# The gate products of a two-layer mixer encoder: seven products in another order, with common sums copied into a second PSUM bank

## The chip, the cores and the metric

The kernel runs on one core of one Trainium2 chip. The metric is the device time of one execution in microseconds (us). The kernel before takes 2005.57 us, the median of 3 runs (2004.29 to 2006.87). One more execution was profiled; all rows below are from it.

## The reference, cut to what matters

Two layers follow one another. In each, `h` is the normalised input (1024 tokens of 1024 channels), four branches give `y_n`, and each branch is weighted by its own gate, a full 1024 x 1024 product with a bias and a sigmoid:

```python
for n, y in enumerate(branch_outs):                     # 4 branches
    y_n = (y * gate_paths[:, :, n]) @ w_branch[n]
    mg = jax.nn.sigmoid(h @ w_gate[n] + b_gate[n])
    merged = mg * y_n if merged is None else merged + mg * y_n
return x + merged @ w_out
```

## The kernel before, in words

All data lie transposed: channels on the 128 partitions, tokens along the free axis, in two halves of 512 tokens (`hf` 0 and 1). A fp32 product is made from three passes: each operand is split into a high and a low part by `split` (ACT copies the high part, DVE subtracts it from the source, lines 104 and 105), and `passes` (line 128) issues high-high, high-low and low-high matmuls of 128 x 128 weights on 512 columns.

`gates` (line 1007) computes the four gate products of a layer. Its outer loop runs over four pairs of output chunks (`dp`), its inner loop over the four branches (`n` in `ORDER`): 16 iterations in a layer, 32 in the kernel. An iteration makes a 2 x 2 block of results (two chunks `d` by two token halves `hf`) by a scheme of Strassen's kind, in the form of Winograd: seven products over four 128-row blocks each in the place of eight. So an iteration has 7 x 4 x 3 = 84 matmuls. The right operands are made once in a layer: `b11`, `b21` and `b22` are parts of `h`, and `tf[1]` to `tf[4]` (called t1 to t4 below) are differences of those parts, made by `token_forms` (t1 and t2 in tiles of tag `M`, t3 in tag `A`, t4 in tag `H`; `h` has tag `H` too). The left operands are made anew in each iteration by the generator `weight_forms` (line 974): two loads of 512 KB (`raw`), sums and differences by DVE (line 981), and a split of each of the seven forms into a `wf` tile, of which there are 6. `product` (line 1022) takes the forms from a list that is kept six ahead of TensorE.

Each iteration has three PSUM banks, G, A and B, taken in one iteration from the pool `mm` (3 banks) and in the next from `aux` (5 banks). The order of the products is

- b11 into G; ACT copies G to `p1` (line 1046)
- t2 into A; DVE adds `p1` to `c6`
- b21 onto G; result (0,0) is read from G
- t1 onto A; DVE adds `p1` to `c65`
- t3 into B; DVE adds B to `c65`, which is result (1,1)
- b22 onto A; DVE adds A to `p1`, which is result (0,1)
- t4 onto B; DVE adds B to `c6`, which is result (1,0)

`weigh` (line 1032) takes a result through the sigmoid (ACT, line 1035), multiplies it with the tile of `y` (DVE) and adds it to the sum over the branches (DVE; not in the first iteration of a `dp`). After a `dp`, `m` is stored through the POOL queue; the last `dp` stays on the chip as the tail. `out_proj` follows: `merged` reads `m` back (`mt`), splits it chunk by chunk (tile `m`, lines 104 and 105), and the products `op` begin with the first token half. The list scheduler of the framework sets the order on each engine, from program order and from what is ready; DMAs and weight loads are raised in priority.

Of the kernel before, what the change touches and what calls it, by code (L numbers as in the profile page):

```python
# [11 lines left out]
AF = mybir.ActivationFunctionType  # L12
ALU = mybir.AluOpType

P = 128
# [30 lines left out]
class Net:  # L46
# [931 lines left out]
    def weight_forms(self, l):  # L978

        nc = self.nc  # L980
        op = lambda o, a, b, f: nc.vector.tensor_tensor(out=o, in0=a, in1=b, op=f)
        flip = 0
        for dp in range(4):
            for n in ORDER:
                raw = self.raw(), self.spare(flip)
                flip = 1 - flip
                ys = [self.slot(f"y{d}", tag="A") for d in range(2)]
                with self.tc.high_priority(offset=AHEAD):
                    for r, d in zip(raw, range(2)):
                        nc.sync.dma_start(out=r, in_=self.a["w_gate"][l, n, 2 * dp + d])  # L990
                    for y, d in zip(ys, range(2)):
                        nc.gpsimd.dma_start(out=y, in_=self.y[l][n, 2 * dp + d])
                a11, a12, a21, a22 = raw[0][:, 0:4], raw[0][:, 4:8], raw[1][:, 0:4], raw[1][:, 4:8]
                yield self.weight_form(a11), ys
                s1, s2 = (self.t2(f"s{j}").rearrange("p (k n) -> p k n", n=P) for j in (1, 2))
                op(s1, a21, a22, ALU.add)
                op(s2, s1, a11, ALU.subtract)
                yield self.weight_form(s2), ys
                yield self.weight_form(a12), ys
                yield self.weight_form(s1), ys  # L1000
                op(a11, a11, a21, ALU.subtract)
                yield self.weight_form(a11), ys
                op(a12, a12, s2, ALU.subtract)
                yield self.weight_form(a12), ys
                yield self.weight_form(a22), ys

    def gates(self, l, tf):

        nc = self.nc
        b11, b21 = [self.h[k] for k in range(4)], [self.h[4 + k] for k in range(4)]  # L1010
        b22 = [[self.h[4 + k][1]] for k in range(4)]
        add = lambda o, a, b: nc.vector.tensor_tensor(out=o, in0=a, in1=b, op=ALU.add)
        flip = 0
        forms, made = self.weight_forms(l), []
        for dp in range(4):
            acc = None
            for i, n in enumerate(ORDER):
                bank = (self.mm, self.aux)[flip]
                flip = 1 - flip
                G, A, B = bank("g"), bank("ga"), bank("gb")  # L1020

                def product(ps, x, first):
                    while len(made) < LEAD:
                        f = next(forms, None)
                        if f is None:
                            break
                        made.append(f)
                    w, ys = made.pop(0)
                    self.passes(ps, [((w[0][:, k], w[1][:, k]), xk[0]) for k, xk in enumerate(x)], True, first, True)
                    return ys  # L1030

                def weigh(c, d, hf, src=None):

                    y = ys[d][:, hf * H:hf * H + H]
                    nc.scalar.activation(out=c, in_=c if src is None else src, func=AF.Sigmoid,
                                         bias=self.p(l, C_BG + 8 * n + 2 * dp + d))
                    if i == 0:
                        nc.vector.tensor_tensor(out=y, in0=y, in1=c, op=ALU.mult)
                    else:
                        nc.vector.tensor_tensor(out=c, in0=y, in1=c, op=ALU.mult)  # L1040
                        a = acc[d][:, hf * H:hf * H + H]
                        add(a, a, c)

                ys = product(G, b11, True)
                p1 = self.t2("p1")
                nc.scalar.activation(out=p1, in_=G, func=AF.Copy)
                product(A, tf[2], True)
                c6 = self.t2("c6")
                add(c6, A, p1)
                product(G, b21, False)  # L1050
                c11 = self.t2("c11")
                weigh(c11, 0, 0, G)
                product(A, tf[1], False)
                c65 = self.t2("c65")
                add(c65, A, p1)
                product(B, tf[3], True)
                add(c65, B, c65)
                weigh(c65, 1, 1)
                product(A, b22, False)
                add(p1, A, p1)  # L1060
                weigh(p1, 0, 1)
                product(B, tf[4], False)
                add(c6, B, c6)
                weigh(c6, 1, 0)
                if i == 0:
                    acc = ys
            if dp < 3:
                for d in range(2):
                    nc.gpsimd.dma_start(out=self.m[l][2 * dp + d], in_=acc[d])
        return acc  # L1070
# [200 lines left out]
```

## Time and profile before

| | before |
|---|---|
| median of 3 runs | 2005.57 us |
| the profiled execution | 2007.35 us |
| its span, from first to last instruction | 2005.6 us |
| TensorE matmul busy | 1967.1 us, 98% of the span |
| VectorE (DVE) busy | 1486.6 us, 74% |
| ScalarE (ACT) busy | 1000.5 us, 50% |

How to read it: a matmul's busy time holds its way through the array, so that successive matmuls overlap and a row's busy time is longer than its share of the stream. The pace is read from the distance of starts. In a row of the timeline, the first number is the start, the second the time from the first start to the last end of the group, `xN` the number of instructions; in square brackets stand the idle time before it and what ended that.

### The profile page before, as it was taken

How to read it: one execution, taken by the hardware profiler on the slowest of the kernel's cores; microseconds unless marked ns; L12 is line 12 of the kernel's file. 1: busy time of each engine (PE TensorE's matmuls, PEld its weight loads, DVE VectorE, ACT ScalarE, POOL GpSimd, SP SyncE). 2: the span in 40 equal slices, each digit the busy share in tenths (PEclk: the TensorE clock that was granted, in tenths of full speed). 3: DMA queues.
4: the chain of work that ended last, by engine and by line, in shares of the span. 5: the costliest groups of instructions: out<-in, count | busy, mean ns of one | idle time of the engine just before them, and what ended most of it. 6: DMA issues, size and time to landing. Idle time of an engine off the chain costs nothing.

```text
span 2005.6 us, 26782 instructions
## 1 busy us (share of the span) xinstructions
PE 1967.1 (98%) x9484; PEld 1625.6 (81%) x9484; DVE 1486.6 (74%) x2740; ACT 1000.5 (50%) x1917; POOL 41.1 (2%) x90
## 2 busy tenths in 40 slices
PE   8999999999999999999999999999999999999997
PEld 6777887887888888887888888888888888888887
DVE  7598878886577777776655888888564877777775
ACT  6335655567574334344421456656775643443441
POOL 0000000000000000000000000000000000000000
PEclk9999999999999999999999999999999999999999
DMA  7244343423774333427421534433248723424443
GB/s 236 77 149 118 108 123 115 127 72 101 265 270 170 135 106 106 156 73 258 157 86 45 158 116 126 131 108 108 82 147 294 274 86 124 135 98 146 166 150 106
DMA packets 129446, 281.08 MB, mean 140 GB/s; under 512 B 32928, under 2 KB 37920, under 8 KB 129312
## 3 DMA queue, kind: packets, MB, share of 16 engines
q1 hardware_dynamic: 118368, 239.52, 37.1%
q0 software_dynamic: 10944, 39.85, 5.9%
q8 instruction: 75, 1.23, 0.3%
q14 instruction: 59, 0.48, 0.1%
HBM read 186.84 MB, written 67.30 MB: 127 GB/s over the span
## 4 chain that ended last, share of the span: by engine, by line
PE 82%; DVE 9%; ACT 4%; DMA 3%; issue 2%; SPq 0%; DVEq 0%; ACTq 0%
PE z L128 25%; PE ga L128 13%; PE g L128 9%; PE op L128 8%; PE gb L128 8%; PE py L128 8%; PE z L255 3%; DVE cv L848 2%; PE pv L128 2%; PE s L465 1%; PE pt L491 1%; DVE w L105 1%; DMA mt<-m 1%; ACT o L522 1%; DVE p L474 1%
## 5 line engine op out<-in xcount | busy, mean ns | idle before, releaser
L128 PE MATMUL z<-h,w 128*128 128x512 f32 x3000 | 744.3, 397 | 2.5 <-DVE gp L609 1.4
L128 PEld LDWEIGHTS z<-h,w 128*128 128x128 f32 x3000 | 546.7, 188 | 111.4 <-DVE gp L609 1.8
L105 DVE TENSOR_TENSOR w<-wr,w 128x1024 fp32r<-128x1024 f32 (+1 forms) x135 | 158.7, 1179 | 109.4 <-ACT w L104 99.6
L104 ACT ACTIVATE w<-wr 128x1024 fp32r<-128x1024 f32 (+1 forms) x135 | 137.7, 1022 | 175.9 <-PE z L128 80.9
L128 PE MATMUL ga<-t,wf 128*128 128x512 f32 x768 | 189.0, 395 | 0.0
L128 PE MATMUL gb<-t,wf 128*128 128x512 f32 x768 | 187.8, 393 | 0.0
L128 PE MATMUL g<-h,wf 128*128 128x512 f32 x768 | 187.1, 393 | 0.0
L128 PE MATMUL op<-m,w 128*128 128x512 f32 (+1 forms) x960 | 181.2, 349 | 2.2 <-DVE m L105 2.2
L128 PE MATMUL py<-g,w 128*128 128x512 f32 x768 | 181.0, 395 | 0.6 <-DVE gp L609 0.5
L848 DVE SCALAR_TENSOR_TENSOR cv<-cv,params 128x512 f32<-128x512 f32 x240 | 179.4, 747 | 2.3
L128 PEld LDWEIGHTS op<-m,w 128*128 128x128 f32 x960 | 153.7, 188 | 28.1 <-DVE m L105 3.5
L128 PEld LDWEIGHTS ga<-t,wf 128*128 128x128 f32 x768 | 144.4, 188 | 33.8
L128 PEld LDWEIGHTS gb<-t,wf 128*128 128x128 f32 x768 | 144.4, 188 | 33.1
L128 PEld LDWEIGHTS py<-g,w 128*128 128x128 f32 x768 | 143.2, 188 | 34.0 <-ACT sg L608 0.9
L128 PEld LDWEIGHTS g<-h,wf 128*128 128x128 f32 x768 | 144.4, 188 | 32.4
L104 ACT ACTIVATE wf<-wr 128x512 fp32r<-128x512 f32 x144 | 90.9, 631 | 131.7 <-issue 48.3
L105 DVE TENSOR_TENSOR wf<-wr,wf 128x512 fp32r<-128x512 f32 x144 | 99.0, 688 | 21.9 <-ACT wf L104 20.8
L479 ACT ACTIVATE p<-p,nm 128x256 f32<-128x256 f32 (+2 forms) x192 | 87.9, 459 | 42.9 <-DVE nm L476 42.5
L128 PE MATMUL ga<-h,wf 128*128 128x512 f32 x384 | 94.2, 395 | 0.0
L104 ACT ACTIVATE wf<-s 128x512 fp32r<-128x512 f32 x64 | 40.5, 632 | 106.7 <-PE gb L128 64.1
L522 ACT ACTIVATE o<-pv 64x128 f32<-64x128 f32 x192 | 67.6, 352 | 48.6 <-PE pv L128 46.7
L128 PEld LDWEIGHTS ga<-h,wf 128*128 128x128 f32 x384 | 72.4, 188 | 16.7
(244 smaller groups left out, 2683.6 us busy)
## 6 DMA issues: line engine op xcount, KB each, us to landing
wr<-in_w_in_dram SPq DMA_DIRECT2D x75, 512.0 KB, 3.8
y<-y SPq DMA_DIRECT2D x128, 256.0 KB, 4.1
y<-y POOLq DMA_DIRECT2D x64, 512.0 KB, 4.8
wr<-in_w_gate_dram SPq DMA_DIRECT2D x48, 512.0 KB, 4.4
wr<-in_w_out_dram SPq DMA_DIRECT2D x32, 512.0 KB, 3.6
rot<-rt SPq DMA_DIRECT2D x192, 64.0 KB, 2.0
cv<-in_w_gate_dram SPq DMA_DIRECT2D x16, 512.0 KB, 4.8
wr<-in_w_branch_dram SPq DMA_DIRECT2D x16, 512.0 KB, 4.5
```

What stands on the lines that cost most here:

```text
L104: self.nc.scalar.activation(out=hi, in_=src, func=AF.Copy)
L105: self.nc.vector.tensor_tensor(out=lo, in0=src, in1=hi.bitcast(F32), op=ALU.subtract)
L128: self.nc.tensor.matmul(ps, w, x, start=(first and i + u == 0), stop=(i == n - 1 and u == 2), skip_group_check=open_)
L255: self.nc.tensor.matmul(ps, a[:, k], b, start=(k + j == 0), stop=(k == KC - 1 and j == 2))
L465: mm(s[i][h], q[h + j][:, qs], k[h][:, a:a + n], start=(j == 0), stop=(j == 2))
L474: nc.vector.tensor_tensor_reduce(out=p[:, h * 256:h * 256 + n], in0=s[h], in1=mask, scale=0.125, scalar=-3.0e38, op0=ALU.add, op1=ALU.max, ...
L479: nc.scalar.activation(out=ph, in_=ph, func=AF.Exp, bias=nm[:, h:h + 1], accum_out=st[:, t, 2 + h:3 + h])
L491: nc.tensor.transpose(pt[:rows[ci], cs], p[:, off:off + rows[ci]], self.ident)
L522: nc.scalar.activation(out=dst, in_=src, func=AF.Copy)
L848: self.tc.keep_in_program_order(nc.vector.scalar_tensor_tensor(out=y, in0=u[:, j:j + H], scalar=tap(j), in1=y, op0=ALU.mult, op1=ALU.add))
```

## The change

The seven products have another order and other banks. X, Y and V come from `mm` in each iteration; `aux` is not used here. ACT copies the sum in X into bank Y, and further matmuls accumulate on Y; the five DVE additions that joined partial sums become two, and ACT gets two more copies. The order after is

- b11 into X; ACT copies X to Y
- t3 into V; ACT copies V to `v7`
- t2 onto Y; ACT copies Y to `u2`
- t4 onto V; DVE adds V to `u2`, which is result (1,0)
- t1 onto Y; DVE adds Y to `v7`, which is result (1,1)
- b21 onto X; result (0,0) is read from X
- b22 onto Y; result (0,1) is read from Y

`weight_forms` yields the forms in the order of the products, and a11 - a21 gets a tile of its own (`s3`) in the place of a11.

```diff
                 a11, a12, a21, a22 = raw[0][:, 0:4], raw[0][:, 4:8], raw[1][:, 0:4], raw[1][:, 4:8]
+                s1, s2, s3 = (self.t2(f"s{j}").rearrange("p (k n) -> p k n", n=P) for j in (1, 2, 3))
                 yield self.weight_form(a11), ys
-                s1, s2 = (self.t2(f"s{j}").rearrange("p (k n) -> p k n", n=P) for j in (1, 2))
+                op(s3, a11, a21, ALU.subtract)
+                yield self.weight_form(s3), ys
                 op(s1, a21, a22, ALU.add)
                 op(s2, s1, a11, ALU.subtract)
                 yield self.weight_form(s2), ys
+                yield self.weight_form(a22), ys
+                yield self.weight_form(s1), ys
                 yield self.weight_form(a12), ys
-                yield self.weight_form(s1), ys
-                op(a11, a11, a21, ALU.subtract)
-                yield self.weight_form(a11), ys
                 op(a12, a12, s2, ALU.subtract)
                 yield self.weight_form(a12), ys
-                yield self.weight_form(a22), ys
...
-        flip = 0
...
-                bank = (self.mm, self.aux)[flip]
-                flip = 1 - flip
-                G, A, B = bank("g"), bank("ga"), bank("gb")
+                X, Y, V = self.mm("g"), self.mm("ga"), self.mm("gb")
...
-                ys = product(G, b11, True)
-                p1 = self.t2("p1")
-                nc.scalar.activation(out=p1, in_=G, func=AF.Copy)
-                product(A, tf[2], True)
-                c6 = self.t2("c6")
-                add(c6, A, p1)
-                product(G, b21, False)
+                copy = lambda o, a: nc.scalar.activation(out=o, in_=a, func=AF.Copy)
+                ys = product(X, b11, True)
+                copy(Y, X)
+                product(V, tf[3], True)
+                v7 = self.t2("v7")
+                copy(v7, V)
+                product(Y, tf[2], False)
+                u2 = self.t2("u2")
+                copy(u2, Y)
+                product(V, tf[4], False)
+                add(u2, V, u2)
+                weigh(u2, 1, 0)
+                product(Y, tf[1], False)
+                add(v7, Y, v7)
+                weigh(v7, 1, 1)
+                product(X, b21, False)
                 c11 = self.t2("c11")
-                weigh(c11, 0, 0, G)
-                product(A, tf[1], False)
-                c65 = self.t2("c65")
-                add(c65, A, p1)
-                product(B, tf[3], True)
-                add(c65, B, c65)
-                weigh(c65, 1, 1)
-                product(A, b22, False)
-                add(p1, A, p1)
-                weigh(p1, 0, 1)
-                product(B, tf[4], False)
-                add(c6, B, c6)
-                weigh(c6, 1, 0)
+                weigh(c11, 0, 0, X)
+                product(Y, b22, False)
+                c12 = self.t2("c12")
+                weigh(c12, 0, 1, Y)
```

## Rows read from the trace of the kernel before

**Rows 1.** The page, part 1: busy time (us), share of the span and number of instructions of an engine.

```profile
PE 1967.1 (98%) x9484; PEld 1625.6 (81%) x9484; DVE 1486.6 (74%) x2740; ACT 1000.5 (50%) x1917; POOL 41.1 (2%) x90
```

**Rows 2.** Busy time by stretch, for the gate stage of layer 0 and of layer 1. The columns are the stretch, its length, then busy time and number of instructions of PE, PEld, DVE, ACT and POOL, then the granted clock (1.00 is full speed), the DMA share and GB/s.

```profile
605.90:917.96 312.06, 312.06 (x1346) 253.06 (x1344) 236.40 (x362) 126.77 (x196) 17.77 (x34) 1.00 0.38 130
1590.70:1900.10 309.40, 309.40 (x1345) 252.39 (x1344) 235.78 (x362) 126.50 (x196) 17.66 (x34) 1.00 0.38 129
```

**Rows 3.** Groups of matmuls of the gate stage (first from the page, over both layers: busy time, mean ns of one, idle time of PE before them), and below them the one wait of PE in the seams behind it, from the waits over the whole span (total, times, longest).

```profile
L128 PE MATMUL ga<-t,wf 128*128 128x512 f32 x768 | 189.0, 395 | 0.0
...
L128 PE MATMUL g<-h,wf 128*128 128x512 f32 x768 | 187.1, 393 | 0.0
...
PE op L128 <- DVE m L105: 2.2, 2, 1.2
```

**Rows 4.** The timeline of PE, one iteration in the middle of layer 0, product by product (b11, t2, b21, t1, t3, b22, t4) and the b11 of the next iteration.

```profile
781.41 2.96 PE L128 MATMUL g<-h,wf 128*128 128x512 f32 x12
784.21 2.96 PE L128 MATMUL ga<-t,wf 128*128 128x512 f32 x12
787.01 2.91 PE L128 MATMUL g<-h,wf 128*128 128x512 f32 x12
789.76 2.95 PE L128 MATMUL ga<-t,wf 128*128 128x512 f32 x12
792.55 2.93 PE L128 MATMUL gb<-t,wf 128*128 128x512 f32 x12
795.32 2.96 PE L128 MATMUL ga<-h,wf 128*128 128x512 f32 x12
798.12 2.96 PE L128 MATMUL gb<-t,wf 128*128 128x512 f32 x12
800.92 2.96 PE L128 MATMUL g<-h,wf 128*128 128x512 f32 x12
```

**Rows 5.** The same for an iteration in the middle of layer 1.

```profile
1745.37 2.91 PE L128 MATMUL g<-h,wf 128*128 128x512 f32 x12
1748.12 2.95 PE L128 MATMUL ga<-t,wf 128*128 128x512 f32 x12
1750.90 2.91 PE L128 MATMUL g<-h,wf 128*128 128x512 f32 x12
1753.66 2.95 PE L128 MATMUL ga<-t,wf 128*128 128x512 f32 x12
1756.44 2.93 PE L128 MATMUL gb<-t,wf 128*128 128x512 f32 x12
1759.21 2.92 PE L128 MATMUL ga<-h,wf 128*128 128x512 f32 x12
1761.97 2.91 PE L128 MATMUL gb<-t,wf 128*128 128x512 f32 x12
1764.72 2.91 PE L128 MATMUL g<-h,wf 128*128 128x512 f32 x12
```

**Rows 6.** The timeline of PE at the beginning of the gate stage of layer 0: the last product of the branches (`py`), then the first b11, t2 and b21.

```profile
599.68 6.39 PE L128 MATMUL py<-g,w 128*128 128x512 f32 x27
605.90 2.92 PE L128 MATMUL g<-h,wf 128*128 128x512 f32 x12
608.66 2.95 PE L128 MATMUL ga<-t,wf 128*128 128x512 f32 x12
611.45 2.91 PE L128 MATMUL g<-h,wf 128*128 128x512 f32 x12
```

**Rows 7.** Groups of instructions of the gate stage of layer 0 (605.7 to 917.7 us), for durations: busy time, mean ns of one, and idle time before them with what ended it. They are the copy of G to SBUF, the sigmoid read from PSUM, a high part of a weight form, and a weight form's sum.

```profile
L1046 ACT ACTIVATE p<-g 128x512 f32<-128x512 f32 x16 | 9.6, 597 | 19.0 <-PE g L128 18.9
L1035 ACT ACTIVATE c<-g,params 128x512 f32<-128x512 f32 x16 | 11.0, 689 | 32.6 <-PE g L128 32.6
L104 ACT ACTIVATE wf<-s 128x512 fp32r<-128x512 f32 x32 | 20.2, 632 | 53.4 <-PE gb L128 32.1 <-DVE s L981 21.3
L981 DVE TENSOR_TENSOR s<-s,wr 128x512 f32<-128x512 f32 x15 | 10.3, 685 | 0.0
```

**Rows 8.** The timeline of ACT and DVE within the iteration of rows 4: the copy of G after b11, and the addition that reads A after t1.

```profile
784.41 0.60 ACT L1046 ACTIVATE p<-g 128x512 f32<-128x512 f32 x1 [1.35 <-PE g L128]
...
793.70 0.68 DVE L1012 TENSOR_TENSOR c<-ga,p 128x512 f32<-128x512 f32 x1
```

**Rows 9.** The timeline at the seam from the gates to `out_proj`: PE in layer 0 and in layer 1, then DVE in layer 0.

```profile
917.96 4.78 PE L128 MATMUL op<-m,w 128*128 128x512 f32 x20
923.75 26.60 PE L128 MATMUL op<-m,w 128*128 128x512 f32 x113 [1.01 <-DVE m L105]
...
1900.14 4.81 PE L128 MATMUL op<-m,w 128*128 128x512 f32 x20
1906.17 43.93 PE L128 MATMUL op<-m,w 128*128 128x512 f32 x205 [1.22 <-DVE m L105]
...
916.97 0.68 DVE L1012 TENSOR_TENSOR p<-ga,p 128x512 f32<-128x512 f32 x1
...
920.03 0.68 DVE L1012 TENSOR_TENSOR c<-gb,c 128x512 f32<-128x512 f32 x1
920.64 0.68 DVE L1012 TENSOR_TENSOR y<-y,p 128x512 f32<-128x512 f32 x1
...
923.01 0.68 DVE L105 TENSOR_TENSOR m<-mt,m 128x512 fp32r<-128x512 f32 x1
```

## The prediction

> **What bounds the kernel now.** I read first the page's busy shares: TensorE's matmuls fill 98% of the span, DVE 74%, ACT 50% [rows 1]. A share over the whole span says little, so the next view is busy time by stretch for the two stages that the change touches. There PE is busy without a gap, at a granted clock of 1.00 (the upper level, 2.4 GHz), for 312.1 and 309.4 us; DVE is busy for 76% of that time and ACT for 41% [rows 2]. The third view is what PE waited for: before the gate matmuls, nothing at all; the only waits near the change are two of `op` in the seams behind the gates, on DVE [rows 3]. So the gate stage is bound by the stream of matmuls alone. Time can come from two places: the pace of that stream, and the seams. Taking work from DVE inside the stage is worth nothing by itself.
>
> The pace is read from the distance of starts in PE's timeline. An iteration of layer 0 takes 800.92 - 781.41 = 19.51 us, one of layer 1 takes 1764.72 - 1745.37 = 19.35 us, with the same 84 matmuls [rows 4, 5]. Per product, in the order of before, layer 0 / layer 1: b11 2.80 / 2.75, t2 2.80 / 2.78, b21 2.75 / 2.76, t1 2.79 / 2.78, t3 2.77 / 2.77, b22 2.80 / 2.76, t4 2.80 / 2.75. This difference is small and it is regular, so I looked for its rule. The operand alone does not decide it: the very first b11 of layer 0, behind the branches' `py`, takes 608.66 - 605.90 = 2.76 [rows 6], and in the later iteration, behind t4, 2.80 [rows 4]. t1 and t2 take 2.78 to 2.80 wherever they stand. b11, b21, b22 and t4 take either 2.75 or 2.80, and what they take is what came before them: right after t1 or t2 (b21) 2.75 in both layers; after t3 (b22) 2.80 in layer 0 and 2.76 in layer 1, and this pace is handed on from b22 to t4 to b11 until t2 ends it. What in the machine does this no row tells.
>
> **The change part by part.**
>
> *Matmuls.* The count stays at 7 x 12 in an iteration. The order becomes b11, t3, t2, t4, t1, b21, b22. If the rule holds, t4 stands behind t2 and b21 behind t1, so both take 2.75; b22 takes over 2.75 from b21, and b11 from b22; t3 no longer stands ahead of a product that could take over its pace, because t2 follows. An iteration is then 4 x 2.75 + 2 x 2.79 + 2.77 = 19.35 us in both layers. Layer 0 gains 16 x (19.51 - 19.35) = 2.6 us, layer 1 nothing. Bounds: all five of b11, t3, t4, b21 and b22 at 2.80 and t1, t2 at 2.80 give 19.60, a loss of 16 x 0.09 + 16 x 0.25 = 5.4 us; t3 at 2.75 as well gives 0.02 x 32 = 0.6 us more gain, 3.2 in all. I take 2.6, since the products behind t1 agree in both layers [rows 4, 5] and behind t1 and t2 is where two of the four now stand.
>
> *DVE.* Three of five additions go, 3 x 32 in all at 0.68 us [rows 8]: 65 us of DVE time that PE never waited for, hence 0 inside the stage [rows 3]. The sum for a11 - a21 is not dropped, it only gets another tile. One more scratch tile is alive in an iteration (seven in place of six, of twelve): 0.
>
> *ACT.* Two copies more, 2 x 32 x 0.60 = 38 us [rows 7], on an engine with 59% of the stage free. No row shows a copy from PSUM into PSUM. The nearest rows are the copy out of PSUM at 0.60 and a copy within SBUF at 0.63 [rows 7]; I take 0.60. What decides is the cover. The copy of G starts 0.20 us after b11's successor has started and ends at 785.01 [rows 8]; the product that needs it is the one after next, at 787.01 [rows 4]. So the copy could take 2.6 us before PE waited. It is hidden, at 0; if the cover were gone, it would cost its whole 0.8 us (0.20 + 0.60) in each iteration, 26 us in all. The copies of V and of Y have the same cover of one product.
>
> *New waits.* Six PE waits are of the same kind: t2 on the copy into Y, t4 on the copy of V, t1 on the copy of Y (ACT); b22 on the addition that reads Y after t1 (DVE); the next b11 and t3 on banks freed by a sigmoid of ACT or an earlier read. Each has one whole product, 2.75 us or more, between the write that is read and the write that waits. Before, t1 waited in the same way for an addition after t2, b22 for one after t1. That last one is the tightest that I found: it starts at 793.70, 1.15 us after t1's successor has started, because DVE had sums of the weight forms to make, and ends at 794.38, 0.94 us ahead of b22 at 795.32 [rows 4, 8]. Behind a PE wait stands all of PE's stream. I cost these waits at 0; the bound is the rival below.
>
> *Weight forms and loads.* The same seven splits and four sums, in another order; the pair a21, a22 is released three products earlier, a11 and a12 one later. The loads on SP and POOL are the same in number and move past no other queue entry by more than that; they have two iterations of buffer, 39 us. 0.
>
> *The seams.* In layer 0, 20 `op` matmuls start at 917.96; at 19.51 / 84 = 0.232 us each the next is due at 922.60, but it starts at 923.75: 1.15 us lost. It waits for a low part of `m` that DVE makes from 923.01 to 923.69, behind the last additions of the gates. In layer 1 the next is due at 1904.78 and starts at 1906.17: 1.39 us [rows 9]. In front of that low part stand two additions that the change removes from the last results, at 916.97 and 920.03; in a run of them the next starts 0.61 later [rows 9], so the low part comes about 1.2 us earlier, and the last result is no longer one of the first token half, which `op` reads first. The loss falls to 0 in layer 0 and to 0.2 in layer 1: gain 1.15 + 1.2 = 2.4 us. Bounds: 0 (another order on DVE, or ACT held by the loads of `mt`) and 2.5. What is late next in the seam is the stream itself.
>
> *Sum.* -2.6 - 2.4 = -5.0 us. Against the profiled execution's own 2007.35 us that is 2002.3; the same difference on the median of the runs, 1.8 us below it, is 2005.57 - 5.0 = 2000.6 us, a gain of 0.25%. I count faster or slower from 0.2%, 4.0 us, about what a measurement of this kernel can tell from no change. So the forecast lies just on the far side of that line.
>
> **The rivals.**
>
> *The pace stays what it is, the seams alone gain.* If the pace hangs on something else than the product before (the tile's place, or a pattern that is set once in a layer), layer 0 keeps 19.51: 2005.57 - 2.4 = 2003.2 us, within 0.2%. For it: no row explains the rule, and layer 1 shows that the same chain of products can run at the other pace. Against it: b11 at 2.76 and 2.80 in the same layer [rows 4, 6].
>
> *Nothing reaches the time.* The scheduler orders the seam so that DVE's low parts wait as long as before, and the pace stays: 2005.6 us.
>
> *Slower: Y is written again before DVE has read it.* b22 must not start before the addition that reads Y after t1 has ended. In program order DVE has, from the end of t4: the addition of V (0.69), a wait for the sigmoid (0.69 on ACT), multiplication and addition (2 x 0.69), two sums for the weight forms (2 x 0.69), and a low part that waits for its high part on ACT (0.63 + 0.69) [rows 7]; with 0.2 us for the start that is 5.7 us, and then the addition itself, to 6.3. b22 is due 2 x 2.77 = 5.5 us after the end of t4. The loss is 0.8 us in an iteration, 32 x 0.8 = 26 us: 2005.57 + 26 - 5 = 2026 us. It decides where the addition starts later than 2.1 us after t1's successor. Against it: in the same place before, with five additions to serve, DVE began it 1.15 us after t1's successor and filled the wait for the sigmoid with a sum [rows 8]. For it: three banks serve all iterations, where before there were six in turn, so no second set takes up a delay.
>
> That stage showed no waits with two sets of banks in turn. The Trainium skill, in "Perfetto Trace Analysis", section "Optimizing Tensor Performance", wants independent matmul groups to rotate through different PSUM banks, so that the evacuation of one overlaps the next group's matmuls; the change halves the banks in rotation, and by that rule this rival's time would be the result. The trace before speaks less for it, with a read that ended 0.94 us early [rows 8].
>
> **How the numbers follow.** The forecast, both gains: 0.46. Seams alone: 0.24. Nothing: 0.14. Slower through Y: 0.13. Slower through the pace (its bound of 5.4, less what the seams give): 0.03. Faster by over 0.2% is the forecast, 0.46; within 0.2% are the second, the third and the pace, 0.41; slower by over 0.2% is the wait on Y, 0.13. The predicted time is that of the likeliest, 2000.6 us. The likeliest alone would lie between 1999 (3.2 and 2.5 gained, 1 us of spread between runs) and 2002. The range that should hold 8 in 10 reaches from 1998.5 over the two cases without a gain to 2007.5 (2005.6 and its spread, or the bad pace of 5.4 less a seam's gain); the wait on Y stays outside.
>
> **What would show it.** Right: iterations of 19.35 us in layer 0 with every t4, b21, b22 and b11 at 2.75; no idle time before gate matmuls; the `op` matmuls of the seam without a gap of over 0.3 us; about 65 us less DVE and 38 us more ACT. Wrong: products of 2.80 behind t1 or t2 (the rule of the pace), a gap of over 1 us left at 922 (the seam), or the same short gap before b22 in every iteration, released by DVE or ACT (the banks).

## The result, and the profile after

The changed kernel takes 2016.3 us (median of 4 runs, 2015.6 to 2018.3) against 2004.93 us for the kernel before (4 runs, 2004.14 to 2006.87). The ratio is 1.0057 with a 95% interval of 1.0039 to 1.0074: slower by 11.4 us, where 5.0 us less were forecast. The profiled execution took 2016.92 us, with a span of 2015.0.

The gate stages came close to what the prediction said. Busy time by stretch in the kernel after, for the gate stages of layer 0 and of layer 1 (columns as in [rows 2]):

```profile
604.82:914.50 309.68, 309.68 (x1345) 252.23 (x1343) 209.06 (x316) 137.50 (x226) 17.76 (x34) 1.00 0.39 128
1593.58:1903.77 310.19, 310.19 (x1345) 252.09 (x1343) 209.15 (x316) 137.48 (x226) 17.77 (x34) 1.00 0.38 126
```

Beside [rows 2], layer 0 went from 312.06 to 309.68, 2.4 us less; layer 1 from 309.40 (309.54 by the first starts of its b11 and its `op`, 1590.60 and 1900.14) to 310.19, some 0.65 us more. PE is busy without a gap, and DVE has 27 us less to do in each layer. The timeline of PE, from one t3 to the next in layer 0 (t3, t2, t4, t1, b21, b22, b11, t3), answers to [rows 4]:

```profile
781.77 2.93 PE L128 MATMUL gb<-t,wf 128*128 128x512 f32 x12
784.54 2.96 PE L128 MATMUL ga<-t,wf 128*128 128x512 f32 x12
787.34 2.91 PE L128 MATMUL gb<-t,wf 128*128 128x512 f32 x12
790.09 2.95 PE L128 MATMUL ga<-t,wf 128*128 128x512 f32 x12
792.88 2.91 PE L128 MATMUL g<-h,wf 128*128 128x512 f32 x12
795.63 2.91 PE L128 MATMUL ga<-h,wf 128*128 128x512 f32 x12
798.38 2.91 PE L128 MATMUL g<-h,wf 128*128 128x512 f32 x12
801.13 2.93 PE L128 MATMUL gb<-t,wf 128*128 128x512 f32 x12
```

t4 behind t2, b21 behind t1, b22 and b11 all take 2.75 us, and an iteration takes 801.13 - 781.77 = 19.36 us, where before it took 19.51.

What was lost was lost in the seams. The timeline of PE there, the last product of the gates and the first `op` of each layer (they answer to [rows 9]):

```profile
911.75 2.91 PE L128 MATMUL ga<-h,wf 128*128 128x512 f32 x12
919.22 31.00 PE L128 MATMUL op<-m,w 128*128 128x512 f32 x121 [4.55 <-ACT m L104]
...
1901.02 2.91 PE L128 MATMUL ga<-h,wf 128*128 128x512 f32 x12
1908.21 51.52 PE L128 MATMUL op<-m,w 128*128 128x512 f32 x225 [4.27 <-ACT m L104]
```

The wait of PE here over the whole span, from the waits of the same kernel (total, count and longest; it answers to the last of [rows 3]):

```profile
PE op L128 <- ACT m L104: 8.8, 2, 4.6
```

PE waits 8.8 us in place of 2.2, and for another engine: ACT, which makes the high parts of `m`. ACT is not busy; its own timeline says what it waited for:

```profile
918.53 3.94 ACT L104 ACTIVATE m<-mt 128x512 fp32r<-128x512 f32 x6 [3.15 <-DMA mt<-m]
```

The loads `mt` stand in SP's queue, whose timeline in the kernel after is:

```profile
901.55 2.23 SPq L1116 DMA_DIRECT2D xn<-in_xT_dram  x5
904.97 0.33 SPq L115 DMA_DIRECT2D wr<-in_w_out_dram  x1
905.35 2.78 SPq L1116 DMA_DIRECT2D xn<-in_xT_dram  x5
910.73 0.33 SPq L115 DMA_DIRECT2D wr<-in_w_out_dram  x1
911.15 1.33 SPq L1116 DMA_DIRECT2D xn<-in_xT_dram  x3
912.54 6.23 SPq L1076 DMA_DIRECT2D mt<-m  x9
```

The same queue in the kernel before:

```profile
902.14 3.65 SPq L1119 DMA_DIRECT2D xn<-in_xT_dram  x8
908.31 0.33 SPq L115 DMA_DIRECT2D wr<-in_w_out_dram  x1
908.73 2.75 SPq L1079 DMA_DIRECT2D mt<-m  x6
```

Before, the six `mt` loads of the first token half went out at 908.73, behind 8 loads of `xn` and 9.2 us ahead of the first `op` [rows 9]. After, they stand behind 13 loads of `xn` and one more weight unit, and go out at 912.54, when the gates have 2 us left. What is late is the issue, not the transfer: over all `mt` loads the median from issue to landing is 5.6 us after and 6.2 before. Nor did SP hold the loads back until a scratch tile came free: between 890 and 925 us the waits of the `mt` line (L1076) on SP are all on other DMAs, 0.9 us at most. They are late by their place in the queue.

A second loss stands behind the first. Busy time by stretch of the kernel after, at and behind the two waits (columns as in [rows 2]; the clock is the number ahead of the last two):

```profile
910.00:920.00 10.00, 5.45 (x23) 3.83 (x21) 7.09 (x11) 4.34 (x7) 0.14 (x2) 0.89 0.99 363
920.00:930.00 10.00, 10.00 (x35) 8.03 (x35) 8.27 (x13) 7.09 (x12) 0.00 (x0) 0.77 0.78 289
...
1905.00:1910.00 5.00, 1.79 (x4) 1.50 (x5) 3.26 (x6) 1.89 (x3) 0.00 (x0) 0.76 0.95 311
1910.00:1915.00 5.00, 5.00 (x14) 3.90 (x13) 4.31 (x8) 4.49 (x8) 0.00 (x0) 0.56 0.93 355
```

The granted clock falls to 0.77 and 0.56 of full speed, a mean of the upper level (2.4 GHz) and the lower one (1.2 GHz); 35 matmuls fill the stretch from 920 to 930 us; e5_filled, below, runs 42 in 9.81 us at 1.00.

### The profile page after: what moved, and what is told of

Read it like the earlier page. It is cut to its first block, busy times and chain, and to the rows that moved or that the text cites. A ratio compares the mean times of both kernels' runs of the same rounds, so it can differ in the third digit from the quotient of the medians.

```text
span 2015.0 us, 26675 instructions
## 1 busy us (share of the span) xinstructions
PE 1971.4 (98%) x9484; PEld 1629.0 (81%) x9484; DVE 1430.8 (71%) x2644; ACT 1023.9 (51%) x1981; POOL 41.1 (2%) x90
## 4 chain that ended last, share of the span: by engine, by line
PE 83%; DVE 8%; ACT 4%; DMA 3%; issue 2%; SPq 0%; DVEq 0%; ACTq 0%
PE z L128 24%; PE ga L128 13%; PE op L128 9%; PE gb L128 9%; PE py L128 9%; PE g L128 8%; PE z L255 3%; DVE cv L848 2%; PE pv L128 2%; PE s L465 1%; PE pt L491 1%; ACT w L104 1%; ACT o L522 1%; DVE w L105 1%; DVE p L474 1%
## 5 line engine op out<-in xcount | busy, mean ns | idle before, releaser
L128 PE MATMUL op<-m,w 128*128 128x512 f32 (+1 forms) x960 | 186.3, 356 | 8.8 <-ACT m L104 8.8
L128 PEld LDWEIGHTS op<-m,w 128*128 128x128 f32 x960 | 157.9, 193 | 36.0 <-ACT m L104 9.7
L105 DVE TENSOR_TENSOR wf<-wr,wf 128x512 fp32r<-128x512 f32 x112 | 77.3, 690 | 85.0 <-ACT wf L104 84.4
L104 ACT ACTIVATE wf<-s 128x512 fp32r<-128x512 f32 x96 | 59.8, 625 | 49.1 <-PE gb L128 49.1
L937 ACT ACTIVATE y<-py 128x512 f32<-128x512 f32 x128 | 70.5, 597 | 27.0 <-PE py L128 24.6
```

The source lines that it names most:

```text
L104: self.nc.scalar.activation(out=hi, in_=src, func=AF.Copy)
L105: self.nc.vector.tensor_tensor(out=lo, in0=src, in1=hi.bitcast(F32), op=ALU.subtract)
L128: self.nc.tensor.matmul(ps, w, x, start=(first and i + u == 0), stop=(i == n - 1 and u == 2), skip_group_check=open_)
L937: self.nc.scalar.activation(out=y, in_=ps, func=AF.Copy)
```

## The experiments

The theory after this result (queue): the last scratch tiles, c11 and c12, are first written behind the last two products; the scheduler orders the `mt` loads, which need scratch tiles of the same tag, behind them; so the loads go out late, `op` waits, and the clock falls. The main rival (banks): `op` waits because the three banks X, Y and V come free late. The pace and the clock had rivals of their own.

**The two last results in old tiles (e1_reuse).**

```diff
-                c11 = self.t2("c11")
-                weigh(c11, 0, 0, X)
+                weigh(u2, 0, 0, X)
...
-                c12 = self.t2("c12")
-                weigh(c12, 0, 1, Y)
+                weigh(v7, 0, 1, Y)
```

> The changed kernel, but the last two results go into the scratch tiles u2 and v7, which are free by then, in place of the fresh tiles c11 and c12. Theory Q (queue): the seam is long because the last fresh scratch tiles are first written behind the last two products, the loads of mt are ordered behind them and land behind the loads of xn and of the fourth weight unit; then the mt loads move forward in SP's order, op starts with less than 0.5 us of idle time in both layers, the granted clock stays at 1.00, the gate stages keep about 309.7 us, and the time is 2000 us (1999 to 2002). Rival B (banks): op waits because X, V and Y are freed late by the last sigmoids; these are as before, so the idle time of over 4 us stays and the time is 2013 to 2017 us.

Measured: 2004.91 us (11 runs) against 2005.37, ratio 1.0002 (0.9993 to 1.0011). The loss of 11 us is gone while the banks are used as before the edit, which rules them out as its cause, but the gain is not there either. SP's queue at the end of layer 0:

```profile
903.42 0.91 SPq L1074 DMA_DIRECT2D mt<-m  x2
905.89 3.05 SPq L1074 DMA_DIRECT2D mt<-m  x5
```

The timeline of DVE and PE there:

```profile
909.99 0.69 DVE L105 TENSOR_TENSOR m<-mt,m 128x512 fp32r<-128x512 f32 x1 [0.64 <-ACT m L104]
...
912.34 0.68 DVE L1012 TENSOR_TENSOR v<-ga,v 128x512 f32<-128x512 f32 x1
913.08 3.02 PE L128 MATMUL ga<-h,wf 128*128 128x512 f32 x12 [0.39 <-DVE v L1012]
```

The `mt` loads moved forward as expected. But now a split of `m` stands on DVE within the last iteration, together with 0.64 us in which DVE waits for ACT's part of it. The addition that reads Y comes at 912.34, 2.8 us after t1's successor has started (909.54), and b22 has to wait for it: 0.39 us, the slower rival of the prediction, in the last iteration of a layer alone. In layer 1 it is 0.40. The expectation of 1999 to 2002 us is missed. The profiled execution of e3_mt_first (below) has a span 3.1 us shorter: 1.7 us of that lie ahead of the gates of layer 0 (605.36 against 603.70), where neither edit changes a line, 0.8 us from there to the gates of layer 1, and 0.6 us behind.

**The kernel before, its last result in a fresh tile (e2_fresh).**

```diff
-                add(c6, B, c6)
-                weigh(c6, 1, 0)
+                c21 = self.t2("c21")
+                add(c21, B, c6)
+                weigh(c21, 1, 0)
```

> The kernel before, with one edit: its last result goes into a fresh scratch tile c21 behind the last product, in place of c6. Same banks, same order of products, same number of instructions. Theory Q: the mt loads fall behind the xn loads, op stands idle for 4 to 5 us in both seams and the granted clock falls behind that; 5 to 6 us in each layer, 2015 to 2017 us. Rival B: nothing changes, 2004 to 2006 us.

Measured: 2016.29 us (4 runs) against 2005.37, ratio 1.0054 (1.004 to 1.0067). One more scratch tile, first written at the end of an iteration, brings nearly the whole loss (10.9 of 11.4 us) into the kernel before, with its order of products, its two sets of banks and its number of additions untouched. SP's queue at the end of layer 0, behind the same 8 loads of `xn` and weight unit as in the kernel before:

```profile
906.31 2.27 SPq L1120 DMA_DIRECT2D xn<-in_xT_dram  x5
911.44 0.33 SPq L115 DMA_DIRECT2D wr<-in_w_out_dram  x1
911.82 1.37 SPq L1120 DMA_DIRECT2D xn<-in_xT_dram  x3
913.29 6.51 SPq L1080 DMA_DIRECT2D mt<-m  x9
```

PE at the two seams:

```profile
920.20 0.51 PE L128 MATMUL op<-m,w 128*128 128x512 f32 x1 [4.50 <-ACT m L104]
...
1906.23 0.50 PE L128 MATMUL op<-m,w 128*128 128x512 f32 x1 [2.63 <-ACT m L104]
```

The clock behind the first, from the busy time by stretch (columns as above):

```profile
920.00:930.00 10.00, 9.58 (x33) 7.51 (x34) 8.63 (x13) 7.92 (x14) 0.00 (x0) 0.83 0.61 229
```

The wait was forecast at 4 to 5 us in both seams; in layer 1 it is 2.63 us, with 1.28 us more behind the first `op` matmul.

**The changed kernel with the `mt` loads first (e3_mt_first).** The fresh tiles stay.

```diff
                 X, Y, V = self.mm("g"), self.mm("ga"), self.mm("gb")
+                if (dp, i) == (3, 3):
+                    self.mts = [self.t2("mt") for _ in range(6)]
+                    for k, t in enumerate(self.mts):
+                        nc.sync.dma_start(out=t, in_=self.m[l][k][:, 0:H])
...
```

In the part cut here, `merged` takes these six tiles for the first token half.

> The changed kernel, fresh tiles and all, but the six mt loads of the first token half are issued ahead of the last iteration of the gates. Theory Q: 1999 to 2002 us, no idle time over 0.5 us before op. Rival B: 2013 to 2017 us.

Measured: 2001.69 us (10 runs) against 2005.37, ratio 0.9982 (0.9973 to 0.9991). By its median this is the fastest version found. The loads go out well ahead of the last iteration, which starts near 894 us. SP's queue in layer 0:

```profile
879.92 5.45 SPq L1021 DMA_DIRECT2D mt<-m  x6
```

PE at the two seams:

```profile
910.63 2.91 PE L128 MATMUL ga<-h,wf 128*128 128x512 f32 x12
913.38 46.84 PE L128 MATMUL op<-m,w 128*128 128x512 f32 x201
...
1895.63 48.58 PE L128 MATMUL op<-m,w 128*128 128x512 f32 x225
```

`op` follows b22 at 2.75 us, without a wait, as the theory expected. Its first 225 matmuls in layer 1 take 48.58 us, where the changed kernel needs 51.52: 2.9 us. In layer 0 they take 46.84 / 201 = 0.233 us each against 31.00 / 121 = 0.256: 121 x 0.023 = 2.8 us.

**The kernel before with the same early loads (e6_before_mt_first).** The edit of e3_mt_first, on the kernel before.

> The kernel before with the six mt loads of the first token half issued ahead of the last iteration of the gates, and nothing else: the control for the same edit on the changed kernel. If the change itself gives nothing and the early loads give all, this is 2001 to 2002 us as well. If the gate pace of layer 0 (2.4 us) belongs to the change, as its trace says, this lies between 2003 and 2005.5 us, with layer 0 iterations of 19.51.

Measured: 2002.96 us (11 runs) against 2005.55, ratio 0.9988 (0.9979 to 0.9997). That lies between the two ranges, at the edge of the second. So of the 0.18% that e3_mt_first gains, 0.12% come from the early loads alone. What is left for the change is 0.06%, with intervals that overlap, so that a gain in time by the change itself is not shown. The traces give it 619.87 us for the two gate stages, in the kernel after as in e3_mt_first, against 312.06 + 309.54 = 621.6 in the kernel before, 1.7 us; e6_before_mt_first keeps the 312.06 of layer 0. Its `op` has no wait in layer 0 and one of 0.74 us on ACT in layer 1, where e3_mt_first has none.

**The pace: tags of t1 and t3 exchanged in the kernel before (e4_tags).**

```diff
-            form(1, "M", b12, b11, b11)
+            form(1, "A", b12, b11, b11)
...
-            form(3, "A", b22, b12, b22)
+            form(3, "M", b22, b12, b22)
```

> The kernel before, with the tags of two operands exchanged: t1 in tag A, t3 in tag M. For the pace of the gate matmuls. Theory P (the tile's place sets a product's pace, and a product on h or t4 goes on at the pace that the one before leaves it): b22 now stands behind an operand in tag M, so b22, t4 and b11 take 2.75 us in layer 0 too; its iteration is 19.35 us in place of 19.51, 2.6 us less in all, 2002 to 2003 us. Rival O (the pace belongs to the operand, or is set once in a layer): 19.51 stays, 2004 to 2006 us.

Measured: 2004.16 us (10 runs, 2000.45 to 2006.22) against 2005.37, ratio 0.9994 (0.9985 to 1.0003): as a time, unclear, and the 2002 to 2003 us of theory P are not reached. The trace decides on the pace. PE from t1, in layer 0 (t1, t3, b22, t4, b11):

```profile
786.05 2.93 PE L128 MATMUL ga<-t,wf 128*128 128x512 f32 x12
788.82 2.97 PE L128 MATMUL gb<-t,wf 128*128 128x512 f32 x12
791.62 2.91 PE L128 MATMUL ga<-h,wf 128*128 128x512 f32 x12
794.37 2.91 PE L128 MATMUL gb<-t,wf 128*128 128x512 f32 x12
797.12 2.91 PE L128 MATMUL g<-h,wf 128*128 128x512 f32 x12
```

t1, now in tag A, takes 788.82 - 786.05 = 2.77 us, and t3, now in tag M, 2.80: they have exchanged their paces of [rows 4] (2.79 and 2.77). b22, behind this t3, takes 794.37 - 791.62 = 2.75 us, and t4 2.75, where both took 2.80 [rows 4]. So it is the tile that an operand lies in, not the operand, that sets a product's pace, and a product on `h` or t4 goes on at the pace it is left. The tag alone is not enough: in layer 1 of the kernel before b22 takes 2.76 behind a t3 in tag A [rows 5]. Which place of its tag a tile has, the traces do not show.

**Three banks in the order of before (e7_before_mm).**

```diff
-                G, A, B = bank("g"), bank("ga"), bank("gb")
+                G, A, B = self.mm("g"), self.mm("ga"), self.mm("gb")
```

> The kernel before with all three banks of each iteration from the pool mm, as in the changed kernel, and the order of before. For the pace and for the rival of the banks. If the pace hangs on the order of operands alone, an iteration of layer 0 stays at 19.51 and one of layer 1 at 19.35; if three banks are too few, PE shows idle time before gate matmuls. I expect no idle time and 2004 to 2007 us.

Measured: 2005.15 us in one run. The b11 of an iteration of layer 0, and the first four matmuls of the next b11:

```profile
779.76 2.96 PE L128 MATMUL g<-h,wf 128*128 128x512 f32 x12
...
799.27 1.10 PE L128 MATMUL g<-h,wf 128*128 128x512 f32 x4
```

The iteration takes 19.51 us with three banks as with six, and no gate matmul waits. In the order of before, three banks neither change the pace nor bring the loss.

**PE kept busy in the seam (e5_filled).** 20 matmuls are added to each layer, and nothing reads them.

```diff
+                    self.lastw = w[0]
...
                 weigh(c12, 0, 1, Y)
+                if (dp, i) == (3, 3):
+                    z = self.aux("fill")
+                    for j in range(20):
+                        nc.tensor.matmul(z, self.lastw[:, j % 4], b11[j % 4][0][0], start=True, stop=True)
```

> The changed kernel with work added that the result does not use: 20 matmuls into a free bank behind the last gate product of each layer, so that PE is busy while op waits for the mt loads. Theory C (clock): the slow op matmuls behind the seams are the lowered granted clock that follows the idle 4.5 us; with PE busy the clock stays at 1.00 or near, the wait itself stays, and 2.5 to 3 us come back in each layer: 2010 to 2012 us. Rival D (the op matmuls behind the seam are slow because they wait for the splits of m): nothing comes back, 2015 to 2018 us.

Measured: 2012.84 us (5 runs) against 2005.55, ratio 1.0032 (1.0019 to 1.0044). The median lies 0.84 us above the range of theory C; against its own kernel before it is 7.3 us slower, where the changed kernel is 11.4. The first `op` still starts at 919.46 and waits for ACT, and the clock behind it stays up. The timeline of PE, in layer 0 and the first `op` of layer 1:

```profile
914.43 4.74 PE L1066 MATMUL fill<-h,wf 128*128 128x512 f32 x20
919.46 0.50 PE L128 MATMUL op<-m,w 128*128 128x512 f32 x1 [0.29 <-ACT m L104]
...
1906.05 0.50 PE L128 MATMUL op<-m,w 128*128 128x512 f32 x1 [0.19 <-ACT m L104]
```

Busy time by stretch behind it:

```profile
920.00:930.00 10.00, 9.81 (x42) 8.00 (x43) 9.72 (x15) 7.30 (x13) 0.00 (x0) 1.00 0.85 308
```

So about 4 us of the loss, 11.4 - 7.3, were the clock that follows the idle time, and came back by work that does nothing. The forecast was 5 to 6 us; part of what is missing is that `op` comes later here: from the end of the gates to the first `op` it is 919.46 - 914.43 = 5.03 us in layer 0 and 4.93 in layer 1, against 4.72 and 4.44 in the changed kernel.

**Tags and early loads together in the kernel before (e8_tags_mt_first).** The edits of e4_tags and e6_before_mt_first.

> The kernel before, order of products and additions as before, with the tags of t1 and t3 exchanged and the mt loads first. If what the change brings is the pace of layer 0 alone, these two edits without the change give the same: 2000 to 2002.5 us, ratio to before 0.998. If the two additions of DVE that the change takes from the seam matter beside that, this is 1 to 2 us slower than the changed kernel with the mt loads first (2001.7).

Measured: 2004.01 us (11 runs, 1999.16 to 2006.26) against 2005.55, ratio 0.9988 (0.998 to 0.9997). The time lies above both ranges of the expectation. It is no faster than the early loads alone, and the spread of its runs, 7 us, is wider than what it was to tell apart; whether the additions of DVE matter in the seam stays open.

## Why the prediction was wrong

**The step that failed** is the seam: "The loss falls to 0 in layer 0 and to 0.2 in layer 1: gain 1.15 + 1.2 = 2.4 us", with the bounds "0 (another order on DVE, or ACT held by the loads of `mt`) and 2.5". The additions did leave DVE, but `op` came to wait for something else: 8.8 us for the high parts of `m`, behind late `mt` loads. The bound at 0 had no reason: I let ACT be held by the `mt` loads only for as long as before. That rested on the step on loads, which held that they "move past no other queue entry by more than that" and costed them at 0. I had looked at the loads of the stage, and not at the queue behind it. The first `mt` loads moved behind five more `xn` loads and a weight unit, 3.8 us later, while the gates ended 3.5 us earlier. The runs show the cause from both sides: e2_fresh brings the wait into the kernel before with one fresh scratch tile at the end, e3_mt_first and e1_reuse take it out of the kernel after. That the scheduler gives out scratch tiles in the order of their first use is how I read this; the runs show where the loads end up, not how it decides. The prediction put a second thing at 0, "One more scratch tile is alive in an iteration", and the runs do not part it from the late first use: e2_fresh takes seven tiles in place of six, and e1_reuse five in place of seven.

The seam gain itself was read from one execution. The kernels that end their gates as the kernel before does show less of that wait in their profiles: 1.4 us over both seams in e4_tags and 1.0 in e7_before_mm, where the kernel before has 2.2 [rows 3].

**How the loss adds up.** In the two profiles, 9.4 us of span: 1.1 less before the gates (605.90 against 604.82), 2.4 less in the gates of layer 0, 6.4 more from there to the gates of layer 1, 0.65 more in those, 5.8 more from there to the end. Of the 12 us behind the gates, waits of PE are 8.8 - 2.2 = 6.6 us [rows 3], and slow matmuls behind them 2.8 + 2.9 = 5.7 us, of which e5_filled returned about 4 in its measured time.

**The pace was right in mechanism, its sum too large.** Layer 0 gained 2.4 us (forecast 2.6) and layer 1 lost 0.65 (forecast 0): 1.7 in place of 2.6. In layer 1, t2 and t1 take 2.80 where I put 2.79, and t3 2.78 to 2.79 where I put 2.77. The rival that the pace stays, with a gain in the seams alone, came out the other way round: the pace of layer 0 changed, and the seams lost. It named the tile's place as a possible cause, and in that it was right: e4_tags shows that the operand's tile sets the pace that the next product takes over.

**DVE and ACT were right at 0.** No gate matmul waits. The copy from PSUM to PSUM, which no row showed, is the fastest of ACT's copies, 582 ns against the 0.60 us taken:

```profile
L1041 ACT ACTIVATE u<-ga 128x512 f32<-128x512 f32 x16 | 9.6, 599 | 26.6 <-PE ga L128 26.6
...
L1041 ACT ACTIVATE ga<-g 128x512 f32<-128x512 f32 x16 | 9.3, 582 | 24.0 <-PE g L128 24.0
```

Over the span DVE has 56 us less (1430.8) and ACT 23 us more (1023.9); 65 and 38 were forecast. The forecasts add up durations, while busy time counts overlapping instructions once (two additions of 0.68 us start 0.61 us apart [rows 9]); that this makes up the whole difference is not shown.

**The rivals.** "Slower: Y is written again before DVE has read it" had the right sign for another reason: in the kernel after no gate matmul waits. It is real all the same: the prediction let it begin where the addition starts later than 2.1 us after t1's successor, and in e1_reuse, where DVE gets other work in the last iteration, it starts 2.8 us after and b22 waits. The Trainium skill's rule on rotating PSUM banks ("Perfetto Trace Analysis", section "Optimizing Tensor Performance") is not borne out here: with three banks in place of six, e7_before_mm shows no wait. Another rule of the Trainium skill, on the same page ("Perfetto Trace Analysis", section "Matmul Optimizations"), would have warned of the second loss: it says that the matmul engine scales its power with use, and that matmuls should run back to back. The traces agree: 0.77 behind a wait of 4.55 us, 1.00 where e5_filled filled it.

## What to carry to other kernels

Where a stage is bound by one engine alone, look at that engine's pace and at the stage's two ends: the gain of this change lay in the pace and its loss at the ends, and neither in the DVE work that it saves. An edit that adds a scratch tile with a late first use can move the loads that take tiles of the same tag; read the DMA queue of the stage behind, and issue the loads that the next stage begins with ahead of the last iteration. A wait of PE of some 4 us costs more than its length, because the granted clock falls behind it; behind the wait of 1.01 us in the kernel before [rows 9] it is 1.00 from 920 to 930 us.

## What the runs showed of the hardware

The pace of 128 x 512 matmuls in an unbroken stream at full clock is not one number: 12 of them take from 2.75 to 2.80 us, by the tile that the operand lies in and by the product ahead (e4_tags), and the difference is handed on through up to three products (b22, t4 and b11 in [rows 4]). Over a layer's gates that is 2.4 us of 312. The start of the gates of layer 0, behind nearly the same instructions, fell between 602.50 (e8_tags_mt_first) and 605.90 us (the kernel before) in the profiled executions; so the spans of a single pair of profiles can't tell 3 us, and only their stretches can be compared.
